# FF2's left-hand Strassen sums formed in the FF1 stage and stored, operands streamed product by product, sets of four groups, and a smaller share for GpSimd

## The chip, the cores and the metric

One core of one Trainium2 chip runs the whole layer for one sequence of 1024 tokens. The metric is the device time in microseconds (us), median of the runs; lower is better.

## The reference

```python
mod = silu(c) @ w_ada + b_ada
shift1, scale1, gate1, shift2, scale2, gate2 = split(mod, 6)
u  = LN0(x) * (1 + scale1) + shift1
m  = token_mixer(u)
x  = LN1(alpha * x + gate1 * m)
u2 = LN0(x) * (1 + scale2) + shift2
f  = square(relu(u2 @ w_ff1)) @ w_ff2
x  = LN2(alpha * x + gate2 * f)
```

The model width is 1024 and the hidden width of the feed-forward is 4096; all is float32. FF1 is the product with `w_ff1`, FF2 that with `w_ff2`.

## The kernel before, in words

The program runs through the adaLN vectors and LN0, the token mixer (about 60 to 440 us), the output projection with LN1, FF1 (635 to 969 us), FF2 (969 to 1282 us), and an end in which a remainder of FF2 and LN2 are done tile by tile.

A float32 product is made of three TensorE passes: each operand is split into a high and a low part (`split`, L196: ScalarE casts the high part at L198, VectorE or GpSimd subtracts for the low part at L199), and `mm3` (L201) does high by high, high by low and low by high (L204 to L206). TensorE is PE in the rows, VectorE is DVE, ScalarE is ACT, GpSimd is POOL and SyncE, which issues the loads and stores, is SP.

Both feed-forward products use seven products of half matrices in place of eight (`ORDER`, `LEFT`, `RIGHT`). `term` (L896) forms the sum of blocks that a product needs (L903), and `operand` (L907) splits it. Which of VectorE and GpSimd does a sum or a low part is told by `pick` (L888), which gives GpSimd a share of the calls: `S_A`, `L_A` = 0.3 in FF1 and `S_B`, `L_B` = 0.2, 0.55 in FF2, for sums and low parts.

FF1 goes in eight chunks of 256 features of each half of the hidden width; of the first three (`EARLY`) the products 1 and 2 run ahead. `hidden` (L947) takes relu squared and stores the four raw blocks of each group of 128 features of both halves to DRAM (L952). There are 16 such groups.

FF2 takes 14 of the groups in sets of 2, 3, 3, 3 and 3 (`SETS`). `load_hidden` (L1015) loads all blocks of a set, hidden ones (tile `rh`, L1021) and those of `w_ff2` (tile `raw`, L1025), at product 5 of the set before. `ff2_operands` (L1027) forms the sums of both sides (`at`, `bt`, or in place) and splits them (`ah`, `al`, `bh`, `bl`), two products ahead. `ff2` (L1036) runs a product: 12 matmuls for each group, into four PSUM banks, and at its end four evictions add them to `yacc` in SBUF (L1052, VectorE; the first touch of each is a ScalarE copy, L1050). Products 1, 6, 7 and 4 use the banks `pj`; 2 uses the banks `mx`, and 5 and 3 share `mx` after it, so that product 5 waits for the evictions of product 2. `collect` (L1055) then makes `yacc * gate2 + alpha * x1` of each tile, in two steps (L1060, L1061), and `final` (L1075) adds the last two groups, 24 matmuls for each of eight token tiles, (L1086), norms, and stores.

The order on each engine comes from a scheduler that works from the order of the program and the sizes of the buffers. At run time each engine takes its instructions in that order, one after the other: one that waits holds up all behind it. Tiles of the pool `raw` have 12 places.

Of the kernel before, what the change touches and what calls it, by code (L numbers as in the profile page):

```python
# [47 lines left out]
# column offsets in w_in  # L48
# [3 lines left out]
def shape_constants():  # L52
    """Tables that depend on shapes alone: rotary angles, decays, masks."""
# [26 lines left out]
def layer_kernel(ctx: ExitStack, tc, x, c, w_ada, b_ada, w_in, ret_norm_w, gla_gate_w, gla_gate_b,  # L80
# [18 lines left out]
    # tags of the pool for rows of tiles: one for each name below, and "S" for all the others  # L99
# [27 lines left out]
    # ---------------------------------------------------------------- constants  # L127
# [651 lines left out]
    # ---------------------------------------------------------------- w_out, rows times the norms' weights, columns times gate1  # L779
# [24 lines left out]
    def normed(parts):  # L804
        """(v - mean) * rstd over the row that `parts` make."""
# [12 lines left out]
    def out_part(t, q):  # L818
        """alpha * x + gate1 * m of a half of a tile's row, and the load of x."""
# [17 lines left out]
    def affine(src, mean, rs, w, b, q):  # L837
        """(src - mean) * rs * w + b, on ACT and GpSimd or on DVE."""
# [308 lines left out]
    for c in range(NC - 2):  # L1147
# [86 lines left out]
```

## Time and profile before

| | before |
|---|---|
| time, median of 3 runs | 1357.39 us (1356.94 to 1359.26) |
| span of the profiled execution | 1354.0 us |
| TensorE busy | 1221.7 us, 90% |
| VectorE busy | 977.8 us, 72% |
| GpSimd busy | 567.8 us, 42% |
| ScalarE busy | 497.8 us, 37% |

The profile shows one execution, and its span lies 3.4 us under the median of the runs. Busy shares are averages over stages; the stretches by stage tell more. Times of instructions count from the start of the span, in us; mean and minimum lengths are in ns.

### The profile page before, as it was taken

How to read it: one execution, taken by the hardware profiler on the slowest of the kernel's cores; microseconds unless marked ns; L12 is line 12 of the kernel's file. 1: busy time of each engine (PE TensorE's matmuls, PEld its weight loads, DVE VectorE, ACT ScalarE, POOL GpSimd, SP SyncE). 2: the span in 40 equal slices, each digit the busy share in tenths (PEclk: the TensorE clock that was granted, in tenths of full speed). 3: DMA queues.
4: the chain of work that ended last, by engine and by line, in shares of the span. 5: the costliest groups of instructions: out<-in, count | busy, mean ns of one | idle time of the engine just before them, and what ended most of it. 6: DMA issues, size and time to landing. Idle time of an engine off the chain costs nothing.

```text
span 1354.0 us, 18066 instructions
## 1 busy us (share of the span) xinstructions
PE 1221.7 (90%) x6515; PEld 1017.7 (75%) x6515; DVE 977.8 (72%) x1618; ACT 497.8 (37%) x875; POOL 567.8 (42%) x429
## 2 busy tenths in 40 slices
PE   4899898979999999999979999999998979797991
PEld 1587787768978999887758888888776868676781
DVE  6884876797678663577795534345669989889998
ACT  4515222212212232234555555556553433333312
POOL 2334333453344320132542222224365857676736
PEclk9999999989999999999989999999999989898896
DMA  9583231121011213262325433333242241413202
GB/s 322 190 293 125 78 102 55 55 55 32 19 37 32 71 55 94 69 221 85 109 79 186 138 110 102 105 114 125 86 140 92 95 140 48 148 40 124 93 32 93
DMA packets 101371, 141.87 MB, mean 105 GB/s; under 512 B 9809, under 2 KB 49954, under 8 KB 101282
## 3 DMA queue, kind: packets, MB, share of 16 engines
q1 hardware_dynamic: 101282, 140.73, 32.0%
q8 instruction: 51, 0.84, 0.3%
q14 instruction: 38, 0.31, 0.1%
HBM read 115.53 MB, written 25.17 MB: 104 GB/s over the span
## 4 chain that ended last, share of the span: by engine, by line
PE 30%; DVE 15%; issue 4%; POOL 2%; ACT 2%; DMA 0%; SPq 0%; DVEq 0%; POOLq 0%; ACTq 0%
PE pj L204 6%; PE pj L206 6%; PE pj L205 6%; PE mx L205 4%; PE mx L204 4%; PE mx L206 4%; DVE yacc L1052 2%; DVE bt L903 1%; DVE al L199 1%; DVE at L903 1%; DVE ulp L199 1%; DVE bl L199 1%; DVE rh L903 1%; DVE bs L1087 1%; DVE yacc L1061 1%
## 5 line engine op out<-in xcount | busy, mean ns | idle before, releaser
L199 POOL TENSOR_TENSOR wl<-st,wh 128x512 fp32r<-128x512 f32 (+1 forms) x60 | 79.0, 1335 | 185.3 <-ACT wh L198 94.5
L205 PE MATMUL pj<-wl,uh 128*128 128x256 f32 (+1 forms) x512 | 146.2, 286 | 1.1 <-POOL wl L199 1.1
L204 PE MATMUL pj<-wh,uh 128*128 128x256 f32 (+1 forms) x512 | 146.7, 287 | 0.0
L206 PE MATMUL pj<-wh,ul 128*128 128x256 f32 (+1 forms) x512 | 145.8, 285 | 0.0
L204 PE MATMUL pj<-bh,ah 128*128 128x512 f32 x256 | 101.4, 396 | 5.4 <-DVE yacc L1052 5.4
L204 PE MATMUL pj<-uhp,w1h 128*128 128x512 f32 x256 | 101.4, 398 | 4.6 <-ACT m L959 3.4
L204 PE MATMUL mx<-bh,ah 128*128 128x512 f32 x200 | 82.0, 410 | 25.9 <-DVE yacc L1052 21.2
L206 PE MATMUL pj<-uhp,w1l 128*128 128x512 f32 x256 | 100.5, 393 | 0.5 <-POOL w1l L199 0.5
L205 PE MATMUL pj<-ulp,w1h 128*128 128x512 f32 x256 | 100.6, 393 | 0.3 <-POOL ulp L199 0.2
L205 PE MATMUL pj<-bl,ah 128*128 128x512 f32 x256 | 100.6, 393 | 0.0
L206 PE MATMUL pj<-bh,al 128*128 128x512 f32 x256 | 100.4, 392 | 0.0
L205 PEld LDWEIGHTS pj<-wl,uh 128*128 128x128 f32 x512 | 98.2, 192 | 1.8 <-POOL wl L199 1.3
L204 PEld LDWEIGHTS pj<-wh,uh 128*128 128x128 f32 x512 | 98.0, 192 | 0.8
L206 PEld LDWEIGHTS pj<-wh,ul 128*128 128x128 f32 x512 | 98.2, 192 | 0.2
L199 POOL TENSOR_TENSOR al<-rh,ah 128x512 fp32r<-128x512 f32 x43 | 67.1, 1573 | 43.7 <-ACT ah L198 26.5
L206 PE MATMUL mx<-uhp,w1l 128*128 128x512 f32 x192 | 76.6, 399 | 6.9 <-DVE w1l L199 6.9
L205 PE MATMUL mx<-bl,ah 128*128 128x512 f32 x200 | 81.0, 405 | 0.2 <-DVE bl L199 0.2
L206 PE MATMUL mx<-bh,al 128*128 128x512 f32 x200 | 80.8, 404 | 0.0
L199 DVE TENSOR_TENSOR w1l<-raw,w1h 128x512 fp32r<-128x512 f32 x59 | 50.0, 851 | 40.6 <-ACT w1h L198 17.0
L205 PE MATMUL mx<-ulp,w1h 128*128 128x512 f32 x192 | 76.4, 398 | 2.6 <-DVE ulp L199 2.6
L199 POOL TENSOR_TENSOR bl<-raw,bh 128x512 fp32r<-128x512 f32 x41 | 65.5, 1609 | 29.5 <-PE pj L205 10.6
L204 PE MATMUL mx<-uhp,w1h 128*128 128x512 f32 x192 | 75.8, 396 | 0.0
(288 smaller groups left out, 3309.3 us busy)
## 6 DMA issues: line engine op xcount, KB each, us to landing
raw<-in_w_ff SPq DMA_DIRECT2D x140, 256.0 KB, 3.1
ada<-in_w_ada SPq DMA_DIRECT2D x96, 256.0 KB, 5.3
rh<-hid SPq DMA_DIRECT2D x64, 256.0 KB, 4.2
st<-in_w_in SPq DMA_DIRECT2D x52, 256.0 KB, 3.0
hid<-m SPq DMA_DIRECT2D x38, 256.0 KB, 2.0
hid<-c SPq DMA_DIRECT2D x26, 256.0 KB, 2.0
x<-in_x SPq DMA_DIRECT2D x16, 256.0 KB, 4.8
st<-in_w_out SPq DMA_DIRECT2D x16, 256.0 KB, 2.9
```

The lines of the kernel that those rows point to most:

```text
L199: (lo_eng or G).tensor_tensor(out=lo, in0=src, in1=hi.bitcast(F32), op=ALU.subtract)
L204: T.matmul(ps, lhsT=lh, rhs=rh, start=first, stop=False, skip_group_check=partial)
L205: T.matmul(ps, lhsT=lh, rhs=rl, start=False, stop=False, skip_group_check=partial)
L206: T.matmul(ps, lhsT=ll, rhs=rh, start=False, stop=last, skip_group_check=partial)
L903: pick(share).tensor_tensor(out=res, in0=blocks[a], in1=blocks[b], op=op)
L1052: V.tensor_tensor(out=yacc[t][q], in0=yacc[t][q], in1=ps, op=ALU.add)
L1061: V.scalar_tensor_tensor(out=y, in0=xr, scalar=ALPHA, in1=y, op0=ALU.mult, op1=ALU.add)
L1087: bn = V.bn_stats(out=bs[:, 6 * q:6 * q + 6], in_=ys[q])
```

## The change

- FF2's left operands are formed in the FF1 stage. `hidden` keeps the blocks of a group and makes the left sums of products 5, 6, 7 and 3 on VectorE (`LEFT2`, new tiles `c`), and `keep_hidden` stores the seven left operands. For the two last groups (`REST`) it stores the four raw blocks as before. For the first three chunks one block is stored, dropped and loaded again. That makes 106 stores of 256 KB in place of 64, and as many loads in FF2.
- FF2 loads operands product by product (`ff2_loads`), three products ahead; a block of `w_ff2` is loaded for the product that uses it first (`FIRST_USE`). A left operand is only split; the sums of the right side remain.
- The sets are 2, 4, 4 and 4 groups. A bank gets 12 matmuls per group of a set and is evicted once per product, so evictions fall from 140 to 112 (on VectorE from 124 to 96).
- GpSimd's shares in FF2 become `S_B`, `L_B` = 0.0, 0.2; in FF1 they stay 0.3 for the first three chunks and become 0 for the others.
- Some loads (those for gate2 and for the collects, and FF2's first ones) are issued after the load before them.

All of TensorE's matmuls stay: 1344 in FF1, 1176 in FF2 and 192 in the remainder.

```diff
-S_B, L_B = 0.2, 0.55
+S_B, L_B = 0.0, 0.2
...
-            src = term(LEFT, i, raw1[c, n], lambda: S(W1S, n="w1t"), S_A)
-            w.append(operand(src, lambda s: S(W1S, F32R, n="w1" + s), L_A))
+            src = term(LEFT, i, raw1[c, n], lambda: S(W1S, n="w1t"), S_A if c < EARLY else 0)
+            w.append(operand(src, lambda s: S(W1S, F32R, n="w1" + s), L_A if c < EARLY else 0))
...
+    def keep_hidden(g, i, v):
+        hid[g, i] = dr.tile([P, HALF], F32, tag=f"h{g}_{i}", name=nm("hid"))
+        nc.sync.dma_start(out=hid[g, i], in_=v)
+    blocks = {}
+    LEFT2 = {i: r if len(r) == 2 or i == 7 else r[:3] + (None,) for i, r in LEFT.items()}
     def hidden(c, hh, th, f, v, src=None):
         A.activation(v, v if src is None else src, AF.Relu)
         A.activation(v, v, AF.Square)
-        d = dr.tile([P, HALF], F32, tag=f"h{c}_{hh}_{th}_{f}", name=nm("hid"))
-        nc.sync.dma_start(out=d, in_=v)
-        hid[16 * hh + 2 * c + f, th] = d
+        g = 2 * c + f
+        b = blocks.setdefault(g, {})
+        b[th, hh] = v
+        if g in REST:
+            keep_hidden(g, (th, hh), v)
+        elif (th, hh) == (0, 0):
+            keep_hidden(g, 1, v)
+            if c < EARLY:
+                del b[0, 0]
+        elif (th, hh) == (1, 1):
+            keep_hidden(g, 4, v)
+        elif (th, hh) == (1, 0):
+            if (0, 0) not in b:
+                b[0, 0] = S(n="c")
+                nc.sync.dma_start(out=b[0, 0], in_=hid[g, 1])
+            for i in (5, 6, 7):
+                keep_hidden(g, i, term(LEFT2, i, b, lambda: S(n="c"), 0))
+        else:
+            keep_hidden(g, 2, v)
+            keep_hidden(g, 3, term(LEFT2, 3, b, lambda: S(n="c"), 0))
...
-    SETS = [2, 3, 3, 3, 3]
+    SETS = [range(0, 2), range(2, 6), range(6, 10), range(10, 14)]
+    FIRST_USE = {1: (0, 0), 2: (1, 0), 5: (0, 1), 6: (1, 1)}
...
-    def load_hidden(g):
...
+    def load_w2(g, hh, q):
+        raw2.setdefault(g, {})[hh, q] = w = raw((P, HALF))
+        f = 16 * hh + g
+        nc.sync.dma_start(out=w, in_=w_ff2[0, f * P:(f + 1) * P, q * HALF:(q + 1) * HALF])
+    def load_hidden(g, i):
+        rawh[g, i] = S(n="rh")
+        last_load[0] = nc.sync.dma_start(out=rawh[g, i], in_=hid[g, i])
+    def ff2_loads(gs, i):
+        for g in gs:
+            load_hidden(g, i)
+            if i in FIRST_USE:
+                load_w2(g, *FIRST_USE[i])
     def ff2_operands(gs, i):
         ops2[gs, i] = []
         for g in gs:
-            a = operand(term(LEFT, i, rawh[g], lambda: S(n="at"), S_B), lambda s: S(dt=F32R, n="a" + s), L_B)
+            a = operand(rawh.pop((g, i)), lambda s: S(dt=F32R, n="a" + s), L_B)
             b = operand(term(RIGHT, i, raw2[g], lambda: S(n="bt"), S_B), lambda s: S(dt=F32R, n="b" + s), L_B)
...
-    for x, (n, i) in enumerate(todo):
-        if x + 2 < len(todo):
-            ff2_operands(sets[todo[x + 2][0]], todo[x + 2][1])
-        ff2(n, sets[n], i)
-        if i == 5:
-            for m in (sets + [gs])[n + 1]:
-                load_hidden(m)
+    for n, (gs, i) in enumerate(todo):
+        if n + 3 < len(todo):
+            ff2_loads(*todo[n + 3])
+        elif n + 3 == len(todo):
+            load_rest()
+        if n + 2 < len(todo):
+            ff2_operands(*todo[n + 2])
+        ff2(gs, i)
```

The first place where the order moves is VectorE within FF2, at the sums of product 5, between a set's evictions (a number behind a name is the tile's own; `pj_` and `mx_` are banks, so a row with one of them into `yacc` is an eviction). Before:

```order
L903 TENSOR_TENSOR at_10664<-rh_10356,rh_10364 128x512
L903 TENSOR_TENSOR rh_10356<-rh_10354,rh_10356 128x512
L199 TENSOR_TENSOR al_10667<-at_10664,ah_10666 128x512
L1052 TENSOR_TENSOR yacc_9562<-yacc_9562,pj_10162 128x512
L903 TENSOR_TENSOR bt_10670<-raw_10360,raw_10358 128x512
L903 TENSOR_TENSOR at_10664<-at_10664,rh_10354 128x512
L1052 TENSOR_TENSOR yacc_9570<-yacc_9570,pj_10163 128x512
L903 TENSOR_TENSOR at_10676<-rh_10372,rh_10380 128x512
L903 TENSOR_TENSOR bt_10670<-raw_10368,bt_10670 128x512
L1052 TENSOR_TENSOR yacc_9578<-yacc_9578,pj_10164 128x512
L903 TENSOR_TENSOR raw_10360<-raw_10368,raw_10360 128x512
```

After the change:

```order
L1085 TENSOR_TENSOR yacc_9392<-yacc_9392,pj_9856 128x512
L199 TENSOR_TENSOR al_9817<-rh_9720,ah_9816 128x512
L903 TENSOR_TENSOR bt_9820<-raw_9722,raw_9584 128x512
L1085 TENSOR_TENSOR yacc_9400<-yacc_9400,pj_9857 128x512
L199 TENSOR_TENSOR al_9827<-rh_9724,ah_9826 128x512
L903 TENSOR_TENSOR bt_9830<-raw_9726,raw_9588 128x512
L903 TENSOR_TENSOR bt_9820<-raw_9802,bt_9820 128x512
L903 TENSOR_TENSOR raw_9722<-raw_9802,raw_9722 128x512
L199 TENSOR_TENSOR bl_9833<-bt_9830,bh_9832 128x512
L1085 TENSOR_TENSOR yacc_9408<-yacc_9408,pj_9858 128x512
L199 TENSOR_TENSOR al_9837<-rh_9728,ah_9836 128x512
L903 TENSOR_TENSOR bt_9840<-raw_9730,raw_9592 128x512
```

The sums of hidden blocks (`at`, `rh`) are gone from between the evictions, and low parts of hidden operands (`al`) and sums of `w_ff2` blocks (`bt`) stand there. The sum into `bt_9820` is the last reader of `raw_9584`, and four rows on the sum for product 6 reads `raw_9802`, a later block.

The second place is SyncE's queue of loads, at the loads of a set. Before, blocks of `w_ff2` and then all the hidden blocks of the next set:

```order
L1025 DMA raw_9820<-in_w_ff 128x512
L1025 DMA raw_9822<-in_w_ff 128x512
L1025 DMA raw_9828<-in_w_ff 128x512
L1025 DMA raw_9830<-in_w_ff 128x512
L1025 DMA raw_9836<-in_w_ff 128x512
L1021 DMA rh_9816<-hid_6700 128x512
L1021 DMA rh_9818<-hid_7462 128x512
L1021 DMA rh_9824<-hid_7506 128x512
L1021 DMA rh_9826<-hid_7418 128x512
```

After the change:

```order
L1052 DMA rh_9800<-hid_7265 128x512
L1052 DMA rh_9804<-hid_7281 128x512
L1052 DMA rh_9808<-hid_7525 128x512
L1052 DMA rh_9812<-hid_7541 128x512
L1048 DMA raw_9802<-in_w_ff 128x512
L1048 DMA raw_9806<-in_w_ff 128x512
L1048 DMA raw_9810<-in_w_ff 128x512
L1048 DMA raw_9814<-in_w_ff 128x512
L1052 DMA rh_9912<-hid_7268 128x512
L1052 DMA rh_9914<-hid_7284 128x512
L1052 DMA rh_9916<-hid_7528 128x512
L1052 DMA rh_9918<-hid_7544 128x512
```

The loads now come in fours, the hidden operands of one product, then its blocks of `w_ff2`, then those of the next product.

The third place is VectorE ahead of the first final addition (`L1086` before, `L1127` in the change). Before:

```order
L1052 TENSOR_TENSOR yacc_9578<-yacc_9578,pj_11240 128x512
L1061 SCALAR_TENSOR_TENSOR yacc_9570<-st_11796,yacc_9570 128x512
L1061 SCALAR_TENSOR_TENSOR yacc_9334<-st_11816,yacc_9334 128x512
L1052 TENSOR_TENSOR yacc_9586<-yacc_9586,pj_11241 128x512
L1061 SCALAR_TENSOR_TENSOR yacc_9578<-st_11804,yacc_9578 128x512
L1060 TENSOR_TENSOR yacc_9586<-yacc_9586,g_1699_7818 128x512
L1061 SCALAR_TENSOR_TENSOR yacc_9586<-st_11812,yacc_9586 128x512
L1086 TENSOR_TENSOR yacc_9202<-yacc_9202,pj_11824 128x512
```

After the change:

```order
L1085 TENSOR_TENSOR yacc_9782<-yacc_9782,pj_11273 128x512
L1094 SCALAR_TENSOR_TENSOR yacc_9774<-st_11956,yacc_9774 128x512
L1094 SCALAR_TENSOR_TENSOR yacc_9528<-st_11984,yacc_9528 128x512
L1094 SCALAR_TENSOR_TENSOR yacc_9782<-st_11964,yacc_9782 128x512
L1085 TENSOR_TENSOR yacc_9790<-yacc_9790,pj_11274 128x512
L1094 SCALAR_TENSOR_TENSOR yacc_9790<-st_11972,yacc_9790 128x512
L1085 TENSOR_TENSOR yacc_9798<-yacc_9798,pj_11275 128x512
L1093 TENSOR_TENSOR yacc_9798<-yacc_9798,g_1753_7934 128x512
L1094 SCALAR_TENSOR_TENSOR yacc_9798<-st_11980,yacc_9798 128x512
L1127 TENSOR_TENSOR yacc_9392<-yacc_9392,pj_11992 128x512
```

In both orders the evictions of the last product (`pj`) and the collects (`L1060`, `L1061` before; `L1093`, `L1094` in the change) stand ahead of it.

## Rows read from the trace of the kernel before

**Rows 1.** The page: the span, and busy time of each engine (share of the span, instructions).

```profile
span 1354.0 us, 18066 instructions
PE 1221.7 (90%) x6515; PEld 1017.7 (75%) x6515; DVE 977.8 (72%) x1618; ACT 497.8 (37%) x875; POOL 567.8 (42%) x429
```

**Rows 2.** Busy time by stretch: start:end, length, each engine, clock, DMA share, GB/s.

```profile
705.00:940.00 235.00, 234.95 (x1027) 192.36 (x1026) 113.92 (x155) 126.93 (x220) 60.83 (x45) 1.00 0.37 124
940.00:969.00 29.00, 25.63 (x105) 20.24 (x104) 22.45 (x22) 14.28 (x26) 14.90 (x10) 0.94 0.36 118
969.00:1000.00 31.00, 30.69 (x132) 24.17 (x131) 12.46 (x15) 18.98 (x35) 13.61 (x10) 1.00 0.49 161
1000.00:1240.00 240.00, 213.12 (x897) 173.44 (x896) 219.74 (x245) 86.74 (x156) 164.48 (x106) 0.94 0.26 85
1282.00:1354.00 72.00, 43.63 (x193) 35.80 (x191) 65.69 (x122) 13.05 (x23) 35.39 (x25) 0.82 0.19 70
```

**Rows 3.** TensorE's timeline in FF2: start, length, line, operation, [idle before <-releaser].

```profile
969.62 0.39 PE L204 MATMUL pj<-bh,ah 128*128 128x512 f32 x1
...
1232.29 0.76 PE L204 MATMUL mx<-bh,ah 128*128 128x512 f32 x1 [6.14 <-DVE yacc L1052]
1232.85 0.63 PE L205 MATMUL mx<-bl,ah 128*128 128x512 f32 x1
1233.28 0.63 PE L206 MATMUL mx<-bh,al 128*128 128x512 f32 x1
...
1266.31 0.39 PE L204 MATMUL mx<-bh,ah 128*128 128x512 f32 x1
...
1273.11 0.39 PE L204 MATMUL mx<-bh,ah 128*128 128x512 f32 x1
...
1325.24 0.39 PE L206 MATMUL mx<-bh,al 128*128 128x512 f32 x1
```

**Rows 4.** Waits of TensorE, 969 to 1282 us: total, times, longest.

```profile
PE mx L204 <- DVE yacc L1052: 21.2, 3, 8.1
PE pj L204 <- DVE yacc L1052: 5.4, 3, 4.4
PE mx L204 <- ACT bh L198: 4.6, 1, 4.6
```

**Rows 5.** Evictions and GpSimd low parts by tile: ns min/median/max, first to last start.

```profile
L1052 DVE TENSOR_TENSOR yacc<-yacc,pj x68: 671/674/691, 996.3 to 1297.2; 128x512 f32<-128x512 f32 x68
L1052 DVE TENSOR_TENSOR yacc<-yacc,mx x56: 672/675/689, 976.7 to 1287.1; 128x512 f32<-128x512 f32 x56
...
L199 POOL TENSOR_TENSOR al<-rh,ah x43: 1282/1715/1832, 925.1 to 1280.2; 128x512 fp32r<-128x512 f32 x43
```

**Rows 6.** VectorE's timeline, 1231 to 1240 us.

```profile
1232.07 0.68 DVE L903 TENSOR_TENSOR rh<-rh,at 128x512 f32<-128x512 f32 x1
1232.67 0.68 DVE L199 TENSOR_TENSOR bl<-bt,bh 128x512 fp32r<-128x512 f32 x1
...
1237.38 1.77 DVE L199 TENSOR_TENSOR bl<-raw,bh 128x512 fp32r<-128x512 f32 x1
1239.08 0.68 DVE L1052 TENSOR_TENSOR yacc<-yacc,mx 128x512 f32<-128x512 f32 x1
```

**Rows 7.** Tile yacc: the final additions, ns min/median/max, first to last start.

```profile
L1086 DVE TENSOR_TENSOR yacc<-yacc,pj x8: 627/628/681, 1299.8 to 1336.5; 128x512 f32<-128x512 f32 x8
L1086 DVE TENSOR_TENSOR yacc<-yacc,mx x8: 670/680/683, 1301.1 to 1340.1; 128x512 f32<-128x512 f32 x8
```

**Rows 8.** The page: DMA issues, count, KB each, us to landing.

```profile
raw<-in_w_ff SPq DMA_DIRECT2D x140, 256.0 KB, 3.1
rh<-hid SPq DMA_DIRECT2D x64, 256.0 KB, 4.2
```

**Rows 9.** Busy time by stretch in the mixer (columns as in rows 2).

```profile
130.00:170.00 40.00, 35.82 (x314) 31.51 (x313) 33.29 (x66) 11.66 (x21) 15.08 (x21) 0.96 0.21 66
180.00:220.00 40.00, 36.24 (x317) 32.10 (x314) 30.94 (x58) 8.25 (x14) 13.98 (x20) 0.96 0.29 85
```

More of the change, by code (lines that the diff above doesn't have):

```diff
@@ L913, in layer_kernel @@
     NC = 8
+    REST = (14, 15)
     W1S = (P, 2, 256)
@@ L917, in layer_kernel @@
     hid = {}
+    last_load = [None]
     def load_ff1(c, hh):
@@ L922, in load_ff1 @@
                 w = raw(W1S)
-                nc.sync.dma_start(out=w, in_=w1v[2 * kh + n, :, :, 2048 * hh + 256 * c:2048 * hh + 256 * (c + 1)])
+                last_load[0] = nc.sync.dma_start(out=w, in_=w1v[2 * kh + n, :, :, 2048 * hh + 256 * c:2048 * hh + 256 * (c + 1)])
                 raw1.setdefault((c, n), {})[hh, kh] = w
@@ L1006, in ff1_rest @@
         yield
-    SETS = [2, 3, 3, 3, 3]
-    NG = D_FF // (2 * P)
+    SETS = [range(0, 2), range(2, 6), range(6, 10), range(10, 14)]
     INTO = {1: (0, 0), 2: (0, 0), 6: (0, 1), 5: (1, 1), 7: (1, 1), 3: (0, 1), 4: (1, 0)}
+    FIRST_USE = {1: (0, 0), 2: (1, 0), 5: (0, 1), 6: (1, 1)}
     rawh, raw2 = {}, {}
@@ L1014, in layer_kernel @@
     yacc = [[None, None] for _ in range(NT)]
-    def load_hidden(g):
-        rawh[g], raw2[g] = {}, {}
-        for hh in range(2):
-            for th in range(2):
-                rawh[g][th, hh] = S(n="rh")
-                nc.sync.dma_start(out=rawh[g][th, hh], in_=hid[16 * hh + g, th])
-            for q in range(2):
-                raw2[g][hh, q] = raw((P, HALF))
-                f = 16 * hh + g
-                nc.sync.dma_start(out=raw2[g][hh, q], in_=w_ff2[0, f * P:(f + 1) * P, q * HALF:(q + 1) * HALF])
+    def load_w2(g, hh, q):
[10 more added lines that the diff above has]
+                load_w2(g, *FIRST_USE[i])
     def ff2_operands(gs, i):
@@ L1034, in layer_kernel, with ff2 @@
     banks = {}
-    def ff2(n, gs, i):
+    def ff2(gs, i):
         ab = ops2.pop((gs, i))
@@ L1064, in layer_kernel, with load_rest, rest_operands @@
     rest = {}
-    def load_rest(g):
+    def load_rest():
+        for g in REST:
+            for hh in range(2):
+                for th in range(2):
+                    load_hidden(g, (th, hh))
+                for q in range(2):
+                    load_w2(g, hh, q)
+    def rest_operands(g):
         for hh in range(2):
             for th in range(2):
-                rest["a", g, hh, th] = operand(rawh[g][th, hh], lambda s: S(dt=F32R, n="a" + s), L_R)
+                rest["a", g, hh, th] = operand(rawh[g, (th, hh)], lambda s: S(dt=F32R, n="a" + s), L_R)
             for q in range(2):
@@ L1073, in load_rest, with final @@
                 rest["b", g, hh, q] = operand(w, lambda s: S(dt=F32R, n="b" + s), L_R)
-    def final(t, gs):
+    def final(t):
         th, o = t // 4, slice((t % 4) * P, (t % 4 + 1) * P)
-        terms = [(g, hh) for g in gs for hh in range(2)]
+        terms = [(g, hh) for g in REST for hh in range(2)]
         ys = yacc[t]
@@ L1155, in layer_kernel @@
             g2 = rowt("g2")
-            for q in range(2):
-                ada(ada_row(5120 + HALF * q, g2[q]))
-            ada(None)
-    sets, g = [], 0
-    for size in SETS:
-        sets.append(range(g, g + size))
-        g += size
-    gs = range(g, NG)
-    todo = [(n, i) for n in range(len(sets)) for i in ORDER]
+            with tc.issue_after(last_load[0].ins):
+                for q in range(2):
+                    ada(ada_row(5120 + HALF * q, g2[q]))
+                ada(None)
+    todo = [(gs, i) for gs in SETS for i in ORDER]
     for h in range(2):
@@ L1171, in layer_kernel @@
     for step, _ in enumerate(ff1_rest(NC - 1)):
-        if step == 0:
-            for m in sets[0]:
-                load_hidden(m)
+        if step in (2, 3, 4):
+            with tc.issue_after(last_load[0].ins):
+                ff2_loads(*todo[step - 2])
         if step in (3, 4):
-            n, i = todo[step - 3]
-            ff2_operands(sets[n], i)
-    for x, (n, i) in enumerate(todo):
-        if x + 2 < len(todo):
-            ff2_operands(sets[todo[x + 2][0]], todo[x + 2][1])
-        ff2(n, sets[n], i)
-        if i == 5:
-            for m in (sets + [gs])[n + 1]:
-                load_hidden(m)
-        if n == len(sets) - 1 and i == 3:
-            for t in range(4):
-                ld = collect(t)
+            ff2_operands(*todo[step - 3])
+    for n, (gs, i) in enumerate(todo):
[6 more added lines that the diff above has]
+        ff2(gs, i)
+        if gs is SETS[-1] and i == 3:
+            with tc.issue_after(last_load[0].ins):
+                for t in range(4):
+                    ld = collect(t)
     with tc.issue_after(ld.ins):
@@ L1190, in layer_kernel @@
         bcast_rows("ln2_b", ln2_b)
-    for m in gs:
-        load_rest(m)
-    for t in range(4, NT):
-        collect(t)
+    for g in REST:
+        rest_operands(g)
+    with tc.issue_after(ld.ins):
+        for t in range(4, NT):
+            collect(t)
     late, later = iter(()), iter(())
     for t in range(NT):
-        tile_steps = final(t, gs)
+        tile_steps = final(t)
         for step in range(4):
```

## The prediction

> **What bounds the kernel now.** I read the page's first lines, then the busy times stage by stage, TensorE's waits, and the timelines where it waits. On the page TensorE is busy for 90% of a span of 1354.0 us [rows 1]; the median of the runs is 1357.39 us, 3.4 above it, and I add those 3.4 at the end. The average hides three regimes [rows 2]. In most of FF1 (705 to 940 us) TensorE is busy for 234.95 of 235 us and VectorE for 113.92: TensorE alone bounds it. In FF2 (1000 to 1240) TensorE is busy for 213.12 of 240 us, VectorE for 219.74. In the last 72 us TensorE is busy for 43.63.
>
> FF2 runs from its first matmul at 969.6 us to the first matmul of the remainder. I count that back from the last matmul (1325.24): the remainder has 192, 0.227 us apart, so 1325.24 − 191 × 0.2272 = 1281.9 us. The 0.2272 is the spacing of an undisturbed run (30 matmuls from 1266.31 to 1273.11) [rows 3]. FF2 thus takes 312.3 us, where its 1176 matmuls need 1176 × 0.2272 = 267.2: **45.1 us are lost**. TensorE's waits name 21.2 + 5.4 us for VectorE's evictions and 4.6 for ScalarE [rows 4], 31.2 in all. The other 13.9 are slow matmuls: behind the wait of 6.14 us they come 0.43 us apart instead of 0.227 [rows 3], the lower of TensorE's two levels (1.2 and 2.4 GHz), and the granted clock of the whole stretch is 0.94 [rows 2]. Without the waits, I expect these to go too.
>
> Why are evictions late? One takes VectorE 0.67 to 0.69 us in all 124 cases, so it is never slow itself; what stands before it in VectorE's order is [rows 5]. A low part is 0.68 us in one place and 1.77 in another, and starts come 0.60 us apart where nothing is stretched, 1.70 where it is [rows 6]. The long ones are operations with two SBUF inputs; an eviction reads one from PSUM. I take it that GpSimd stretches them: its own low parts vary too, 1282 to 1832 ns [rows 5]. The price per GpSimd operation: from 1000 to 1240 us VectorE did 245 operations, 245 × 0.60 = 147.0 us if nothing stretched them; it was busy for 219.74, so 72.7 too many beside 106 GpSimd operations [rows 2], **0.69 us each**. Of the rows here none shows VectorE on this work with GpSimd silent, so this price is an inference.
>
> The Trainium skill (SBUF — State Buffer, "Who interferes with whom") states that a VectorE instruction with two SBUF inputs and a GpSimd one exclude each other, the second being blocked wholly. The kind agrees [rows 5, 6]. By full blocking, each of 145 operations would cost the shortest 1.28 us, and 206 + 145 × 1.28 = 392 us would not fit into the 330 that FF2 had; so the measured 0.69 decides.
>
> **The change part by part.**
>
> *VectorE's load in FF2 and the remainder.* Counted in the two orders (operands, sums, evictions, collects): 343 operations on VectorE and 145 on GpSimd before, 348 and 56 after. The left sums leave (they are formed in FF1), sets of four need 96 evictions on VectorE instead of 124, and in return most low parts come over from GpSimd. Before: 343 × 0.60 + 145 × 0.69 = 306 us, against 330 us from 969.6 to the first final addition at 1299.8 [rows 3, 7]: 93% full, and in bursts more. After: 348 × 0.60 + 56 × 0.69 = 247 us. Per group and seven products TensorE needs 84 × 0.2272 = 19.1 us. VectorE needed about 306/16 = 19.1, a dead heat, and now needs 247/16 = 15.5. VectorE stops being the bound, and the 45.1 us should mostly go.
>
> *Waits that stay or come.* (a) Product 5's sum of two w_ff2 blocks now frees the place for a block of product 6, and VectorE, which works in order, stands at product 6's sum until that block has landed: 3.1 us from issue [rows 8], with evictions queued behind it. There are 12 such places (four groups in three sets). About four rows, 2.4 us, separate freeing and use; I take 1.5 us each, the 0.7 that is left and as much again for the issue, 18 us of VectorE's time; it has 267 − 247 = 20 us of slack, and TensorE has up to two products of lead. (b) Product 5 still waits for the evictions of product 2, whose four banks it takes. I keep 10 us of stalls, between 0 (all slack absorbs) and 30 (two thirds stay); 10 because the load falls by a fifth and it is the load that made evictions late. **FF2: −45 + 10 = −35.**
>
> *Loads.* Hidden loads rise from 64 to 106, 42 × 256 KB more, at 4.2 us from issue to landing, issued three products ahead (33 us) [rows 8]. The w_ff2 loads stay at 256 KB each. The queues move 85 GB/s in FF2 against 161 at its start [rows 2]: room enough, nothing. The issue of a load can wait on SyncE's queue behind one whose place is not free; the order shows the next product's loads behind the last one's, one product apart, so nothing.
>
> *FF1's added work.* 56 left sums, and from GpSimd 18 low parts and 8 sums of w_ff1 (counted in the orders): 82 × 0.60 = 49 us more for VectorE, less 26 × 0.69 = 18 for the GpSimd operations gone. VectorE has 235 − 114 = 121 us free there [rows 2]: covered. If the cover failed in bursts, TensorE would wait for weights. 42 more stores of 256 KB and six reloads go beside. Taken as 0; bounds 0 to +5.
>
> *FF1/FF2 boundary.* From 940 to 969 us TensorE is idle for 29.00 − 25.63 = 3.4 us [rows 2]. First loads and operands now come in steps: −2 (0 to −5).
>
> *The end.* The first final addition came at 1299.8 us, 17.8 after FF2's end at 1281.9, and each tile's after it 5.2 to 5.6 us apart (1299.8 to 1336.5 in seven steps, 1301.1 to 1340.1 in the other bank) [rows 7], TensorE's pace for 24 matmuls, 5.45. Before that addition stood evictions and collects in VectorE's order. After the change, 41 VectorE and about 11 GpSimd operations stand between product 4's last low part and it: 41 × 0.60 + 11 × 0.69 = 32 us, and that low part is due some 27 us before FF2's end (operands are made two products ahead, a product is 48 × 0.2272 = 10.9 us, and I allow two and a half). So the addition comes about 5 us after FF2's end, not 17.8: −13 at most; the eight tiles then run at TensorE's pace with their steps on VectorE, so I take **−9** (0 to −15).
>
> *The mixer.* The order shifts slightly there; its two halves had TensorE busy for 35.82 and 36.24 of 40 us [rows 9], so 0, ±2.5 by their difference over some six such stretches.
>
> Sum: −35 − 2 − 9 = −46: a span of 1308, and 1308 + 3.4 = **1311 us**.
>
> **The rivals.** 0.2%, 2.7 us, is about what a measurement of this kernel can tell from no change.
>
> *Half the gain.* The waits of (a) hit the evictions, and sums come in bursts at product 5 (five sums in the twelve rows that the order shows there). Then about 30 us of stalls stay, and the end gains little: 1357 − 45 + 30 − 2 − 9 = 1331, up to 1350. For it: 12 raw places hold exactly three blocks for each of four groups. Against: loads of a block land in 3.1 us. Chance 0.20.
>
> *Nothing.* GpSimd is not what stretches VectorE. Then the mean duration moves along: 219.74/245 = 0.897 us × 348 = 312 us against 306, and the time stays at about 1357. Against: VectorE's operations are stretched or not as a whole [rows 6], which a slow engine would not show, and GpSimd's vary likewise [rows 5]. Chance 0.04.
>
> *Slower.* Larger sets make the operands of a product a third larger, and SBUF then holds three products' worth: one in use and two ahead, with loads needing places from the same pool. If only one product of look-ahead is left, each product begins with a landing (4.2 us [rows 8]), a cast and a low part (0.68 on VectorE [rows 6], and I allow 0.6 for the cast): 5.5 us. The point from which it decides is (45 + 9)/5.5 = 10 of 28 products; at 21 (all but the first set) it gives 1311 + 21 × 5.5 = 1426. For it: FF2's places are reused after 140 to 144 matmuls, just three products. Against: three products are 33 us, and a chain of 5.5 fits. Chance 0.09.
>
> **How the numbers follow.** The forecast, 1311, gets 0.67: from 1299 (all stalls go, the end gains 15) to 1325. Half the gain 0.20, nothing 0.04, slower 0.09. The range: 1298 to 1340, which takes in most of the second case. Faster by over 0.2%: 0.67 + 0.20, less a little, is 0.86; within 0.2%: 0.05; slower: 0.09.
>
> **What would show it.** Right: VectorE's low parts near 0.68 us; TensorE's waits for evictions in FF2 under 10 us in sum, against 26.6; FF2 shorter than 285 us; granted clock near 1.0; first final addition within 8 us of FF2's end. FF1's length would stay at that of before. Wrong: two-input operations on VectorE still at 1.77 us with few GpSimd operations beside them (then nothing); VectorE waiting for w_ff2 loads, TensorE for evictions behind them (half); TensorE waiting for ScalarE's casts and those for hidden loads at each product's start (slower); or FF1 longer, TensorE waiting there for w1l.

## The result, and the profile after

The change takes 1324.47 us (median of 4 runs, 1322.46 to 1327.16) against 1357.16 (4 runs, 1355.6 to 1359.26): a ratio of 0.9763, 95% interval 0.9744 to 0.9783. That is 32.7 us less, where 46 were forecast (1311); the time lies in the range. The profiled execution is the slowest of the four, with a span of 1325.4 us, 28.6 under that of before.

The table has the stages of each kernel in this study, in us. FF1 begins at its first matmul, FF2 runs from its first matmul to the remainder's first. That one is counted back from the last matmul as in the prediction for before, the change, e1 and e4, and is the 192nd from the end in the others; in those four the two ways differ by at most 0.8 us.

| kernel | FF1 begins | FF1 | FF2 | FF2's end to first final addition | from there to the end | span |
|---|---|---|---|---|---|---|
| before | 635.0 | 334.6 | 312.3 | 17.8 | 54.2 | 1354.0 |
| the change | 647.0 | 337.7 | 268.7 | 17.6 | 54.4 | 1325.4 |
| e1 change, gate2 loads not held | 640.1 | 336.8 | 267.9 | 17.7 | 54.5 | 1316.9 |
| e2 before, gate2 loads held | 644.7 | 342.0 | 312.9 | 15.7 | 54.1 | 1369.4 |
| e3 before, new FF2 share | 641.3 | 330.6 | 275.9 | 26.2 | 49.3 | 1323.3 |
| e4 change, old FF2 share | 647.6 | 337.5 | 285.7 | 15.0 | 54.3 | 1340.1 |
| e5 = e1, left sums in FF2 | 638.9 | 330.7 | 277.7 | 16.9 | 54.0 | 1318.3 |
| e6 = e1, sets of three | 641.3 | 336.8 | 270.8 | 19.3 | 54.5 | 1322.6 |
| e7 = e1, remainder's share 0 | 638.0 | 336.8 | 268.0 | 8.8 | 52.4 | 1303.9 |
| e8 = e1, no reloads | 636.6 | 336.9 | 268.5 | 16.5 | 54.3 | 1312.8 |
| e9 = e7, last tiles off GpSimd | 638.0 | 337.7 | 268.0 | 8.8 | 49.5 | 1301.9 |
| e10 = e7, FF2 off GpSimd | 633.7 | 336.3 | 267.4 | 12.0 | 52.7 | 1302.1 |
| e11 before, both shares | 638.1 | 330.6 | 274.2 | 22.6 | 53.1 | 1318.6 |

FF2 gave 43.6 us; FF1 began 12.0 later and took 3.1 more; the end gave nothing: −43.6 + 12.0 + 3.1 − 0.0 = −28.5, the difference of the spans but for rounding.

The change's page, its span and busy times (as [rows 1]):

```profile
span 1325.4 us, 18122 instructions
PE 1218.9 (92%) x6515; PEld 1021.0 (77%) x6515; DVE 968.9 (73%) x1714; ACT 495.1 (37%) x875; POOL 384.8 (29%) x305
```

VectorE's total hardly moved (968.9 us against 977.8), though it has 96 instructions more; GpSimd's fell from 567.8 to 384.8. The change's busy times by stretch (columns as in [rows 2]; first a stretch of the mixer, then FF1, then FF2 and the end):

```profile
180.00:500.00 320.00, 290.07 (x1964) 258.30 (x1961) 226.70 (x496) 67.94 (x116) 122.19 (x110) 0.93 0.13 36
705.00:940.00 235.00, 229.15 (x990) 186.37 (x990) 167.72 (x252) 122.18 (x214) 23.78 (x16) 0.99 0.55 185
1010.00:1225.00 215.00, 214.18 (x944) 176.69 (x943) 184.83 (x263) 93.10 (x172) 59.88 (x37) 1.00 0.49 163
1225.00:1253.40 28.40, 28.40 (x127) 23.50 (x126) 27.73 (x34) 8.95 (x17) 14.67 (x9) 1.00 0.51 180
1271.00:1325.40 54.40, 26.22 (x116) 21.39 (x114) 48.01 (x100) 13.05 (x23) 29.20 (x21) 0.79 0.21 78
```

In FF2 TensorE is busy for 214.18 of 215 us at a granted clock of 1.00, where it was 213.12 of 240 at 0.94 [rows 2], and VectorE has 30 us idle. In FF1 TensorE lost 5.85 of 235 us, where it lost 0.05. The waits of TensorE from 600 us to the end (as [rows 4]):

```profile
PE mx L206 <- DVE w1l L199: 6.6, 1, 6.6
PE pj L204 <- DVE m L990: 5.9, 2, 4.8
PE mx L205 <- DVE ulp L199: 3.5, 2, 2.5
PE mx L204 <- ACT bh L198: 0.7, 1, 0.7
PE pj L205 <- POOL bl L199: 0.5, 1, 0.5
```

The first three lie in FF1. The first and the third come at its beginning, where they stood before too, the first at 6.9 us:

```profile
PE mx L206 <- DVE w1l L199: 6.9, 1, 6.9
PE mx L205 <- DVE ulp L199: 2.6, 2, 2.4
PE pj L204 <- ACT m L959: 3.4, 2, 1.8
```

New is the second, 5.9 us between 705 and 940 us, for an addition to `m` that frees a bank. Gone is the wait for ScalarE that stood at FF1's end before, the last line here. Of the 26.6 us for evictions in FF2 [rows 4] nothing is left.

### The profile page after: what moved, and what is told of

The parts are those of the page before. It is cut to its first block, busy times and chain, and to the rows that moved or that the text cites. A ratio compares the mean times of both kernels' runs of the same rounds, so it can differ in the third digit from the quotient of the medians.

```text
span 1325.4 us, 18122 instructions
## 1 busy us (share of the span) xinstructions
PE 1218.9 (92%) x6515; PEld 1021.0 (77%) x6515; DVE 968.9 (73%) x1714; ACT 495.1 (37%) x875; POOL 384.8 (29%) x305
## 5 line engine op out<-in xcount | busy, mean ns | idle before, releaser
L199 POOL TENSOR_TENSOR al<-rh,ah 128x512 fp32r<-128x512 f32 x24 | 36.5, 1522 | 267.2 <-DMA rh<-hid 160.5
L198 ACT CAST ah<-rh 128x512 fp32r<-128x512 f32 x106 | 65.1, 618 | 60.6 <-PE mx L206 23.9
L205 PE MATMUL mx<-bl,ah 128*128 128x512 f32 x200 | 77.9, 390 | 0.1
L204 PE MATMUL mx<-bh,ah 128*128 128x512 f32 x200 | 77.1, 390 | 0.7 <-ACT bh L198 0.7
L206 PE MATMUL mx<-bh,al 128*128 128x512 f32 x200 | 77.6, 389 | 0.0
L199 DVE TENSOR_TENSOR w1l<-raw,w1h 128x512 fp32r<-128x512 f32 x73 | 56.9, 783 | 26.3 <-ACT w1h L198 25.1
```

Of the source, the lines that this page charges most:

```text
L204: T.matmul(ps, lhsT=lh, rhs=rh, start=first, stop=False, skip_group_check=partial)
L205: T.matmul(ps, lhsT=lh, rhs=rl, start=False, stop=False, skip_group_check=partial)
L206: T.matmul(ps, lhsT=ll, rhs=rh, start=False, stop=last, skip_group_check=partial)
```

## The experiments

They come in three groups, each on one chip with its own runs of the kernel before: e1 to e4 (before 1358.73 us), e5 to e8 (1360.04), e9 to e11 (1359.54). A ratio is to that one, so kernels of different groups are compared by their ratios.

### e1 and e2: the hold on the gate2 loads

Nothing in the mixer's code is touched, yet it ended 12 us later. The one edit that reaches it is that the loads of `w_ada` for gate2 are held behind FF1's loads. Before, they come during the mixer, and the 16 operations that sum them stand among the mixer's on VectorE. e1 undoes the hold in the change, e2 adds it to the kernel before.

```diff
 # e1; e2 is the reverse, in the kernel before
-            with tc.issue_after(last_load[0].ins):
-                for q in range(2):
-                    ada(ada_row(5120 + HALF * q, g2[q]))
-                ada(None)
+            for q in range(2):
+                ada(ada_row(5120 + HALF * q, g2[q]))
+            ada(None)
```

> The change without the one hold that puts the gate2 loads of w_ada behind FF1's loads; the order of every engine ahead of FF1 is then that of before, and the sums of these 16 loaded blocks stand among the mixer's work on VectorE again. Theory (the hold is what reorders the mixer, and the 12.0 us by which FF1 began later come from that order alone): FF1's first matmul back at 635 us (634 to 636.5), the time at 1324.5 - 12 = 1312 (1309 to 1316). Rival 1 (the mixer was late by the clock of that one execution, not by its order): FF1 begins anywhere between 640 and 648 and the time stays within 1321 to 1328. Rival 2 (the gate2 loads now collide with the loads of FF1 or the mixer): FF1 begins at 635 but takes 5 us or more longer than its 337.7.

> The kernel before with that hold alone added; ahead of FF1 every engine's order is that of the change. Theory (the mixer's order costs 12 us wherever it stands): FF1's first matmul at 647 (645.5 to 648.5), the time 1357 + 12 = 1369 (1365 to 1373). Rival 1 (clock of one execution): 1354 to 1361.

e1: 1317.12 us (1312.92 to 1318.75), ratio 0.9682 (0.9657 to 0.9708), below the change's interval. e2: 1372.55 (1368.57 to 1374.16), ratio 1.0096 (1.0072 to 1.012), slower by 1%. FF1's matmuls, first and last start, in the profiles of before, e1 and e2:

```profile
L204 PE MATMUL pj<-uhp,w1h x256: 388/389/793, 635.0 to 968.9; 128*128 128x512 f32 x128
```

```profile
L204 PE MATMUL pj<-uhp,w1h x256: 388/389/793, 640.1 to 976.2; 128*128 128x512 f32 x128
```

```profile
L204 PE MATMUL pj<-uhp,w1h x256: 388/389/791, 644.7 to 986.1; 128*128 128x512 f32 x128
```

FF1 began neither at 635 in e1 nor at 647 in e2: e1's 640.1 is where rival 1 had it, though its time of 1317 is not. The table settles it: in the ten profiles without the hold FF1 begins at 633.7 to 641.3, mean 638.1; in the three with it at 644.7 to 647.6, mean 646.4. The two don't overlap, so the hold costs some **8.3 us** ahead of FF1, and the profile of before, at 635.0, was an early one: 3.7 of the 12 us are spread between executions. The stretch from 180 to 500 us, in before, e1 and e2:

```profile
180.00:500.00 320.00, 294.07 (x2088) 262.36 (x2085) 240.54 (x522) 73.39 (x125) 129.49 (x116) 0.97 0.19 54
```

```profile
180.00:500.00 320.00, 293.90 (x2028) 261.09 (x2027) 236.21 (x516) 71.64 (x122) 125.76 (x114) 0.95 0.18 52
```

```profile
180.00:500.00 320.00, 290.59 (x1991) 258.69 (x1989) 228.06 (x499) 69.01 (x118) 122.40 (x111) 0.94 0.13 36
```

With the hold TensorE gets through 37 matmuls fewer than in e1, but e1 itself gets through 60 fewer than before with the same order of instructions. So a stretch of time can't tell the hold from the spread. Counting by matmuls can: 3767 stand ahead of FF1 in every kernel. From the 2001st to the 3201st the ten profiles without the hold take 171.6 to 173.9 us and the three with it 176.7 to 179.6, some 5.6 us more; from there to FF1 all thirteen take 109.3 or 109.4. These 1200 matmuls before and in the change:

```profile
352.60:525.70 173.10, 166.63 (x1203) 156.38 (x1202) 111.16 (x283) 42.99 (x73) 55.45 (x39) 0.99 0.16 48
```

```profile
358.10:537.70 179.60, 169.98 (x1203) 159.16 (x1202) 110.30 (x274) 44.41 (x76) 57.39 (x40) 0.97 0.18 52
```

So two thirds of the 8.3 us are lost in the later part of the mixer and what follows it, in the change half as idle time (9.6 us against 6.5) and half as longer busy time at a granted clock of 0.97 against 0.99. The rest lies ahead of them, where the executions without the hold differ among themselves by more. The order around the missing sums is another one on every engine, on TensorE from its 977th matmul on. Which of these moves costs most was not tried. In e2 the hold also costs FF1 7.4 us (342.0), where the sums then run: between 705 and 940 us TensorE waits 3.0 us for one of them and 3.7 for additions to `m`, neither of which it did before. In the change it costs FF1 only 0.9 (337.7 against e1's 336.8).

### e3 and e4: GpSimd's share of FF2 alone

```diff
 # e3: the kernel before; e4: the reverse, in the change
-S_B, L_B = 0.2, 0.55
+S_B, L_B = 0.0, 0.2
```

> The kernel before with GpSimd's shares of the FF2 work at 0.0 and 0.2 in place of 0.2 and 0.55, nothing else. About 83 to 89 operations go from GpSimd to VectorE: some 430 on VectorE and 56 on GpSimd. Theory (0.60 us for an operation of VectorE, 0.69 more for each of GpSimd): 430 x 0.60 + 56 x 0.69 = 297 us against 306, nearly the same load, so 1346 to 1358. Rival A (a GpSimd operation blocks VectorE for its whole 1.28 us): the load falls by 89 x (1.28 - 0.60) = 60 us, FF2 goes to TensorE's 267, the time to 1315 to 1325. Rival B (GpSimd does not stretch VectorE, 0.897 us an operation whatever runs beside): 430 x 0.897 = 386 us against 308, slower by 60 to 80 us: 1417 to 1437.

> The change with FF2's old shares for GpSimd, 0.2 and 0.55: some 273 operations on VectorE and 131 on GpSimd in FF2 and the remainder. Theory (0.69 each): 273 x 0.60 + 131 x 0.69 = 254 us against 247, still under TensorE's 267: 1323 to 1334, so the smaller share gave little and the sums and evictions that left VectorE gave the gain. Rival A (full blocking, 1.28): 273 x 0.60 + 131 x 1.28 = 332 us, slower by 50 to 65 us: 1375 to 1390. Rival B (the share is the whole gain): about 1357.

e3: 1321.70 us (1315.4 to 1325.54), ratio 0.9722 (0.9688 to 0.9756). e4: 1337.04 (1334.18 to 1341.86), ratio 0.9843 (0.9815 to 0.9871). My theory failed for e3 by 24 us and for e4 by a little: this one line, in the kernel before, is worth as much as the whole change (37.0 us against 32.7). FF2's length in the four combinations:

| FF2, us | old share | new share |
|---|---|---|
| sums, sets and loads of before | 312.3 | 275.9 |
| those of the change | 285.7 | 268.7 |

Either remedy takes most of the 45 us, and together they reach TensorE's 267.2. e3's stretch of FF2, and its two-input low parts on VectorE:

```profile
1000.00:1220.00 220.00, 217.04 (x948) 177.04 (x947) 215.96 (x321) 88.39 (x158) 58.81 (x35) 1.00 0.30 100
```

```profile
L199 DVE TENSOR_TENSOR bl<-raw,bh 128x512 fp32r<-128x512 f32 x45 | 39.1, 869 | 1.2 <-ACT bh L198 0.6 <-POOL al L199 0.6
L199 DVE TENSOR_TENSOR al<-rh,ah 128x512 fp32r<-128x512 f32 x43 | 33.6, 783 | 0.0
```

VectorE does 321 operations in 220 us where it did 245 in 240, and its groups take 783 and 869 ns on average. The mean price of a GpSimd operation is as before: (215.96 − 321 × 0.60)/35 = 0.67 us. e4's stretch:

```profile
1010.00:1230.00 220.00, 211.74 (x912) 172.45 (x911) 173.97 (x188) 89.57 (x166) 157.53 (x101) 0.98 0.44 151
```

gives (173.97 − 188 × 0.60)/101 = 0.61, and the change (184.83 − 263 × 0.60)/37 = 0.73. So 0.69 was right as a mean, and full blocking (rival A) is out as a mean, though e3's time is the one that rival A gave. What was wrong is to use the mean for moving an operation. By it, a low part that goes from GpSimd to VectorE changes VectorE's load by 0.60 − 0.69, next to nothing. Some 90 moved, and FF2 fell by 36.4 us, 0.40 each. Where both engines have work without a break, one operation of each takes 1.70 us [rows 6], and both on VectorE 1.20: 0.50 saved. I formed this theory from e3 and tested it in e7.

### e5 and e6: what the left sums and the sets are worth with the new share

```diff
 # e5: in e1; hidden() stores four raw blocks a group
-            load_hidden(g, i)
+            for k in LEFT_USE.get(i, ()):
+                load_hidden(g, k)
+                left.setdefault(g, {})[k] = rawh[g, k]
...
-            a = operand(rawh.pop((g, i)), lambda s: S(dt=F32R, n="a" + s), L_B)
+            a = operand(term(LEFT, i, left[g], lambda: S(n="at"), S_B), lambda s: S(dt=F32R, n="a" + s), L_B)
```

```diff
 # e6: in e1
-    SETS = [range(0, 2), range(2, 6), range(6, 10), range(10, 14)]
+    SETS = [range(0, 2), range(2, 5), range(5, 8), range(8, 11), range(11, 14)]
```

> The change without the g2 hold and with the left sums formed in FF2 again (four raw blocks stored per group, 64 stores; sets, streaming and shares as in the change): 56 sums more on VectorE in FF2, 56 fewer in FF1. Theory (with the small GpSimd share FF2 already stands at TensorE's limit, so the sums' place is worth little): VectorE's load in FF2 and remainder 247 + 56 x 0.60 = 281 us against some 285 that it has there; FF2 from 268 to 268-278, FF1 back from 336.7 to 331-335, the time within 1312 to 1327. Rival (the sums' move carries the gain): FF2 290 or longer, the time 1335 or more.

> The change without the g2 hold and with the sets 2, 3, 3, 3, 3 again: 28 evictions more on VectorE, 17 us, 264 in all against TensorE's 267. Theory: FF2 stays at 268 to 272, the time at 1314 to 1323. Rival (evictions carry the gain): FF2 280 or longer, the time 1328 or more.

e5: 1319.87 us (1314.14 to 1324.67), ratio 0.9705 (0.9665 to 0.9745). e6: 1319.25 (1316.58 to 1324.4), ratio 0.9707 (0.9669 to 0.9745). Both theories hold. The left sums in FF2, with the loads and stores that go with them, cost it 9.8 us (277.7 against 267.9) and give FF1 back 6.1 (330.7 against 336.8). Sets of three cost FF2 2.9 us. The two don't add up: from e3's 275.9 to the change's 268.7 all of the rewrite together gives 7.2. In time neither can be told from e1: the intervals overlap.

### e7: the remainder's share, a test of the price

```diff
 # in e1
-S_R, L_R = 0.4, 0.4
+S_R, L_R = 0.0, 0.0
```

> The change without the g2 hold and with GpSimd's share of the remainder's operands and of the collects at 0 in place of 0.4: 16 operations go from GpSimd to VectorE, in the stretch in which VectorE is saturated (about 28 us before FF2's end to the first final addition). Theory (where VectorE has no idle time a GpSimd operation costs it 1.10 us, an own one 0.60): 16 x 0.5 = 8 us sooner, so the first final addition at 17.8 - 8 = 10 us after FF2's end (8 to 13), and the time 5 to 9 lower, 1308 to 1313. Rival (mean price 0.69): 16 x 0.09 = 1.4 us, no difference: addition at 16 to 18, 1315 to 1319.

1305.49 us (1304.19 to 1314.54), ratio 0.962 (0.957 to 0.9669). Its stretch before FF2's end, and its first final additions:

```profile
1215.00:1242.70 27.70, 27.70 (x124) 22.94 (x123) 27.70 (x46) 9.66 (x18) 2.93 (x1) 1.00 0.57 190
```

```profile
L1127 DVE TENSOR_TENSOR yacc<-yacc,pj x8: 625/628/674, 1251.5 to 1286.8; 128x512 f32<-128x512 f32 x8
```

In 27.7 us VectorE does 46 operations there; in the change it did 34 in 28.4, with 9 of GpSimd beside them. The first final addition comes 8.8 us after FF2's end in place of 17.7: 8.9 us for 16 operations, **0.55 us each**. The addition falls into the theory's range (0.50 each, 8 to 13), the mean price (no difference) is out; the time is 2.5 us under the forecast. But not all of the 8.9 us is what the theory priced. Two waits of VectorE in e1, in the 46 us ahead of its first final addition, for a load and for a collect on GpSimd, are not in e7:

```profile
1221.41 0.69 DVE L1094 SCALAR_TENSOR_TENSOR yacc<-st,yacc 128x512 f32<-128x512 f32 x1 [1.47 <-DMA st<-x1d]
1259.74 0.69 DVE L1094 SCALAR_TENSOR_TENSOR yacc<-st,yacc 128x512 f32<-128x512 f32 x1 [1.40 <-POOL yacc L1093]
```

Without these 2.9 us, stretching alone gives about 6 us, 0.37 an operation, somewhat less than the theory has and four times the mean price's 0.09.

### e8: the reloads

```diff
 # in e1
-            if c < EARLY:
-                del b[0, 0]
```

> The change without the g2 hold, the blocks of the first three chunks kept in SBUF in place of stored, dropped and loaded again. Theory (VectorE stands at a left sum for such a reload, and an addition that frees a bank is late behind it): the wait of TensorE for that addition, 5.7 us in FF1, goes to under 2, and FF1 from 336.7 to 331-334; the time 3 to 5 lower. Rival (the left sums themselves, 56 operations, make VectorE late): the wait stays at 4 to 6, FF1 at 336 to 338.

1315.79 us (1312.84 to 1317.32), ratio 0.9674 (0.9643 to 0.9705), not to be told from e1. TensorE's waits in its FF1:

```profile
PE mx L206 <- DVE w1l L199: 6.9, 1, 6.9
PE pj L204 <- DVE m L988: 6.0, 2, 4.9
PE mx L205 <- DVE ulp L199: 2.8, 2, 2.5
```

The theory fell: FF1 took 336.9, and the wait for the addition that frees a bank (`m`) stayed at 6.0 us. It is not the reloads. With the left sums back in FF2 (e5) that wait was half as long, which speaks for the sums; e5 also takes away 42 stores, and the two were not tried apart:

```profile
PE pj L204 <- DVE m L974: 2.8, 2, 1.7
```

### e9 to e11: GpSimd silent

e9 takes GpSimd out of the last tiles' norm, on top of e7; e10 takes it out of FF2, on top of e7; e11 is the kernel before with the two pairs of constants alone.

```diff
 # e9: in e7
-                (G if q == 0 and t < NT - 1 else V).tensor_tensor(out=r, in0=r, in1=w, op=ALU.mult)
-                (G if t < NT - 1 else V).tensor_tensor(out=r, in0=r, in1=b, op=ALU.add)
+                V.tensor_tensor(out=r, in0=r, in1=w, op=ALU.mult)
+                V.tensor_tensor(out=r, in0=r, in1=b, op=ALU.add)
```

```diff
 # e10: in e7
-S_B, L_B = 0.0, 0.2
+S_B, L_B = 0.0, 0.0
```

```diff
 # e11: in the kernel before
-S_B, L_B = 0.2, 0.55
-S_R, L_R = 0.4, 0.4
+S_B, L_B = 0.0, 0.2
+S_R, L_R = 0.0, 0.0
```

> e7 with the norm's products and sums of GpSimd in the last tiles (3 a tile, 21) on VectorE too. In e7 the small operations of VectorE (128x1, 0.15 us where nothing is stretched) take 1.15, 0.85 and 0.72 us beside GpSimd there, 2.3 us more a tile. Theory: 3 x 0.60 = 1.8 us more a tile, 2.3 less: the stretch from first final addition to the end goes from 52.4 to 48-52, the time 0 to 5 lower than e7's. Rival (VectorE's order is the bound there and three more operations a tile cost their 1.8 us each tile): 62 to 67 us, the time 10 to 15 higher.

> e7 with GpSimd's share of FF2's low parts at 0 too: no GpSimd operation in FF2. Theory (GpSimd is what stretches VectorE): every two-input operation of VectorE in FF2 at 0.68 to 0.70 us on average (before 0.95 to 1.6 by group, in e7 0.68 to 0.92), VectorE busy for 0.60 us an operation; the time within 6 of e7's, since TensorE bounds FF2 already. Rival (something else stretches it, DMA writes into SBUF for one): low parts of VectorE still at 0.75 us or more on average.

> The kernel before with constants alone: S_B, L_B = 0.0, 0.2 (as e3) and S_R, L_R = 0.0, 0.0 (as e7). Theory (VectorE saturated from FF2 to the first final addition, 14 to 16 operations x 0.5 us): 7 to 8 lower than e3, 1311 to 1317. Rival (mean price): as e3, 1319 to 1325.

e9: **1302.40 us** (1300.53 to 1303.65), ratio 0.9576 (0.9543 to 0.9608), the fastest of all, though its interval overlaps e7's. Its last stretch is 49.5 us against 52.4, with 21 more operations on VectorE in it. One of VectorE's small operations there, over the whole of e7 and then of e9 (ns min/median/max):

```profile
L186 DVE TENSOR_TENSOR qt<-qt,qv x26: 132/160/1280, 15.6 to 1294.4; 128x1 f32<-128x1 f32 x24, 128x4 f32<-128x4 f32 x2
```

```profile
L186 DVE TENSOR_TENSOR qt<-qt,qv x26: 134/159/161, 16.1 to 1292.9; 128x1 f32<-128x1 f32 x24, 128x4 f32<-128x4 f32 x2
```

An operation of 0.16 us took up to 1.28 us beside GpSimd, and never more than 161 ns with GpSimd out of the last tiles.

e10: 1307.12 us (1303.93 to 1311.54), ratio 0.9614 (0.9573 to 0.9654). Its FF2 takes 267.4 us, TensorE's own 267.2 by the prediction. The first final addition comes later than in e7, 12.0 us after FF2's end against 8.8; all the low parts are VectorE's now. Two groups of VectorE in it, and a stretch:

```profile
L199 DVE TENSOR_TENSOR al<-rh,ah 128x512 fp32r<-128x512 f32 x98 | 67.0, 684 | 6.4 <-ACT ah L198 4.6 <-PE pj L205 1.2 <-PE mx L205 0.5
L199 DVE TENSOR_TENSOR bl<-raw,bh 128x512 fp32r<-128x512 f32 x71 | 48.7, 685 | 0.8 <-issue 0.2 <-PE pj L206 0.2
```

```profile
1000.00:1215.00 215.00, 214.45 (x947) 177.27 (x946) 186.28 (x303) 90.68 (x166) 0.00 (x0) 1.00 0.48 162
```

With GpSimd silent and the DMA as busy as in the change, the means are 684 and 685 ns, and VectorE's busy time is 186.28/303 = 0.615 us an operation. So GpSimd is what stretched them; the inference of the prediction is now shown. The Trainium skill (SBUF — State Buffer, "Who interferes with whom") calls the pair of ports that VectorE and GpSimd share an exclusive lock, for which a VectorE instruction with two SBUF inputs contends with a GpSimd one that reads SBUF. For a single pair the runs agree (0.60 becomes 1.70 us, and 0.16 becomes 1.28, the length of GpSimd's shortest low part [rows 5]). As a mean cost for each GpSimd operation 0.61 to 0.73 us were measured, or 0.53 to 0.65 if e10's 0.615 us stands for an operation of VectorE that nothing stretches.

e11: 1317.53 us (1314.61 to 1321.56), ratio 0.9684 (0.9638 to 0.973). The addition comes 3.6 us sooner after FF2's end than in e3 (22.6 against 26.2), between the theory's 8 and the rival's 1; the times of e3 and e11 overlap. That stays open. But two pairs of constants in the old kernel gave 1317.5, less than the whole change's 1324.5 and the same as e1's 1317.1. With the same constants the rewrite without the hold is at 1305.5 (e7); the intervals of the two ratios just overlap (0.957 to 0.9669 and 0.9638 to 0.973), so what the rewrite adds to the constants is some 9 us by the ratios, and not certain.

## Why the prediction was right or wrong

The span was forecast at 1308 us and came to 1325.4, 17.4 more: FF2 gained 8.6 more than the term for it, the mixer cost 12.0, FF1 and its boundary 5.1 more, and the end 9 more than their terms. That the time lies in the range is partly luck, since FF2's surplus hid much of the mixer's loss and the range reached up to 1340 for another case, stalls in FF2.

**VectorE bounds FF2, and relief takes it to TensorE's limit: right.** 312.3 became 268.7 us, with no wait for an eviction, the clock at 1.00, and shorter low parts, though at 0.82 and 0.85 us they are not near the 0.68 that was to show it. VectorE's groups of low parts in FF2, before (1000 to 1240 us) and in the change (1010 to 1225 us), with count, busy us and mean ns:

```profile
L199 DVE TENSOR_TENSOR bl<-raw,bh 128x512 fp32r<-128x512 f32 x26 | 29.8, 1155 | 4.4 <-POOL al L199 3.1 <-ACT bh L198 1.3
L199 DVE TENSOR_TENSOR al<-rh,ah 128x512 fp32r<-128x512 f32 x23 | 22.6, 994 | 2.5 <-ACT ah L198 2.5
```

```profile
L199 DVE TENSOR_TENSOR al<-rh,ah 128x512 fp32r<-128x512 f32 x66 | 53.8, 816 | 2.9 <-PE mx L206 1.4 <-ACT ah L198 0.8 <-PE mx L205 0.4
L199 DVE TENSOR_TENSOR bl<-raw,bh 128x512 fp32r<-128x512 f32 x46 | 39.1, 852 | 3.1 <-POOL al L199 2.1 <-ACT bh L198 0.9
```

**Kept stalls of 10 us: too many**, 1.5 were left (268.7 − 267.2). (The rows give a spacing of 6.80/30 = 0.2267 us and not 0.2272, so TensorE's own time is 266.6 and 2.1 were left.) The cause I gave, VectorE standing at the sums of product 6 until a block of `w_ff2` lands, did not come: in the change's waits of VectorE in FF2 such a block is waited for once, by the remainder's scaling.

```profile
DVE raw L1113 <- DMA raw<-in_w_ff: 2.5, 1, 2.5
```

The half-gain rival fell with it, and the slower one too: TensorE waited for no hidden load and 0.7 us for a cast.

**The working inside the term: wrong.** The load sum priced a moved low part at 0.60 − 0.69, so it credited the missing evictions and sums. e3 shows that the share alone gives 36.4 of the 43.6 us; all the rest gives 7.2 on top of it.

**The mixer, 0 ± 2.5: the step that failed most.** The term was set at nothing, and the stage cost 12.0 us in this pair of profiles, 8.3 by all of them. I saw the order shift there and took it for harmless, with a bound from two neighbouring halves of one execution. The hold was named in the change, and its effect was not priced at all.

**FF1's added work, 0 to +5, and the boundary, −2: the boundary right, the added work outside its bound.** TensorE's wait at FF1's end, 3.4 us before, is gone; e3 shows that the new share takes it away (FF1 330.6 against 334.6). The left sums, with their stores and reloads, cost 6.1 us (e1 against e5), a little over the bound. I argued from VectorE's free time, and it was 71% busy in FF1, not full; but it works in order, and an addition to `m` came late. Together +3.1 in the change, where −2 was forecast.

**The end, −9: wrong.** The first final addition came 17.6 us after FF2's end, as before (17.8). I had product 4's last low part 27 us ahead of that end and 32 us of work behind it. The change's timeline of VectorE:

```profile
1232.84 0.69 DVE L199 TENSOR_TENSOR al<-rh,ah 128x512 fp32r<-128x512 f32 x1
...
1254.40 1.77 DVE L199 TENSOR_TENSOR bl<-raw,bh 128x512 fp32r<-128x512 f32 x1
1256.09 1.77 DVE L1094 SCALAR_TENSOR_TENSOR yacc<-st,yacc 128x512 f32<-128x512 f32 x1
...
1265.65 0.69 DVE L1094 SCALAR_TENSOR_TENSOR yacc<-st,yacc 128x512 f32<-128x512 f32 x1 [1.19 <-POOL yacc L1093]
...
1268.34 0.69 DVE L1094 SCALAR_TENSOR_TENSOR yacc<-st,yacc 128x512 f32<-128x512 f32 x1 [1.40 <-POOL yacc L1093]
...
1271.00 0.68 DVE L1127 TENSOR_TENSOR yacc<-yacc,pj 128x512 f32<-128x512 f32 x1
```

That low part came 20.6 us ahead (1253.4 − 1232.8), and the work took 38.2 us (1271.0 − 1232.8). So 6.4 of the 12.6 us that the addition came later than forecast are the guess of two and a half products ahead. The other 6.2 are the price: the 41 operations at 0.60 make 24.6 us, and the 13.6 beside them are stretched operations of 1.77 us and 2.6 us of waits for collects on GpSimd, where 11 × 0.69 = 8 were forecast. That is the mean price again, in a stretch where VectorE is full.

## What to carry to other kernels

Where two engines share a resource, price a moved operation in the stretch where the slower one is full (0.37 to 0.55 us saved here, without and with the waits that go with it), not by the mean over all (0.69 us a GpSimd operation, which made the move look worth nothing). Then try the constant alone, because here it was worth as much as the whole change. A hold on some loads moves all that is ordered by them: look for a stage whose code is not touched and whose order is, and time it by itself.

## What was not expected of the hardware

VectorE's smallest operations suffer most beside GpSimd, for their length: one of 128x1 takes 0.16 us alone and took up to 1.28. And with one order of instructions on the four compute engines, the time to reach FF1 still varied by 7.6 us between executions (633.7 to 641.3), which a single profile on each side takes for an effect of the change.
